# One hybrid-trunk kernel: gate/up groups on pairs of PSUM banks, row scale moved to the end

## The chip, the cores and the metric

The kernel runs on one core of one Trainium2 chip. Its time is the device time of one execution in microseconds; the kernel before took 948.93 us in the median of three runs (948.30 to 949.33). The profile is of one execution of its own. PE is the matrix engine, DVE the vector engine, ACT the scalar engine, POOL the general one; SP only issues DMAs.

## The reference

Two layers over 256 tokens of width 1024, in float32. Each layer has a feed-forward block (FFN), a mixer (attention inside the stream and into 256 memory rows) and a second FFN, with a residual each:

```python
def rmsnorm(x, g):
    y = x * lax.rsqrt(jnp.mean(x * x, axis=-1, keepdims=True) + EPS)
    return y * g

def swiglu(h, w_gate, w_up, w_down):
    return (jax.nn.silu(h @ w_gate) * (h @ w_up)) @ w_down

for i in range(DEPTH):                              # 2 layers
    x = x + 0.5 * swiglu(rmsnorm(x, ffn1_norm[i]), ...)   # 1024 -> 2816 -> 1024
    ...                                             # mixer: in-projection, attention, out-projection
    x = x + 0.5 * swiglu(rmsnorm(x, ffn2_norm[i]), ...)
```

The row factor of the norm, one number r for each token, commutes with the products: silu(r * (xg @ w_gate)) * (r * (xg @ w_up)) is what the FFN needs, and a factor of a row may also be put on after the down product.

## The kernel before

The 256 tokens are two blocks (`tb`) of 128. Every weight is split into a float32r high part and a remainder (L367 on ACT, L385 on DVE), and a product of float32 accuracy is three passes over PE: high x high, high x low, low x high (L542, L545, L548 in `dense`, L565 and L571 in `two_phases`). Normed activations are split likewise. Some products of the FFN are done by a seven-product scheme (`product`, `pair_sums`, `seven`) to save passes.

The order of all work is written out by a small planner, `Flow`: threads are generators that give up control until a planned time or a condition, and instructions are emitted in the order in which the planner runs them. That order is each engine's program order; on the chip an engine runs its queue in that order, and semaphores make an instruction wait for its inputs and for the last readers of what it overwrites. The planner counts resources. A resource is given back, in its count, at the moment the last reader is emitted.

An FFN runs over 11 groups of 256 hidden columns. `plain_chunk` (L845) computes gate and up of a group for both blocks: 512 columns in one PSUM bank per block, 24 passes each. It takes two banks and spawns `evac`. Two neighbouring groups of every FFN go through the seven-product scheme instead and reach `evac` as sums in SBUF; so 4 x 9 = 36 groups are plain and 8 are not. `evac` (L719) does for each block a silu on ACT with scale r (L728), the product with the up half on DVE with scale r (L731) and a 32x32 block transpose on DVE (L739). Then the group goes through DRAM to bring hidden columns onto the partitions (L745, L751) and is split again (L760, L762). The down products sum into four accumulator banks (`Acc`, `down`); `finish` (L688) adds them into x with the factor 0.5 (L694), `seven_sums` (L805) and `end_sums` (L975) add the rest. `prep_rstd` (L674) makes r, ending in a power on POOL (L585).

PSUM has eight banks of 128x512 float32. `banks` is a count of eight, each use is a tile of a pool of eight buffers, and the pool decides which buffer a tile gets. In the mixer many short uses follow one another: scores (`S`), transposed probabilities (`ptp`, in `p_transpose`, L1492), outputs (`AV`), transposed outputs and queries (`otp`, `qmtp`, `qktp`), and between them the projections (`pj`). `p_transpose` emits ACT's copy, gives its bank and returns, and the next head's call takes a bank:

```python
            nc.scalar.copy(out=pt.rearrange("p a b c -> p (a b) c"), in_=tp[:, 0:2 * nb, :])
            t = flow.act(2 * nk)
            banks.give()
```

Of the kernel before, what the change touches and what calls it, by code (L numbers as in the profile page):

```python
# [20 lines left out]
P = 128  # L21
# [144 lines left out]

@with_exitstack
def kernel(
# [34 lines left out]
    def bank(name, shape=(P, 4, P)):  # L203
        return banks.take(list(shape), F32, name)
# [39 lines left out]
    def gain_columns():  # L244
        grow = const.tile([NGC - 16, P], F32, name="grow")
        for src, r0 in ((mix_norm, GC_MIX), (mem_norm, GC_MEM), (ffn2_norm, GC_FFN2)):
            later(grow[r0 - 16:r0, :], src.rearrange("l (k p) -> (l k) p", p=P))
        for src, r0, n in ((mem_q_norm, GC_MQ, 2), (mem_k_norm, GC_MK, 2), (a_q_norm, GC_AQ, 1),
                           (a_k_norm, GC_AK, 1)):
            for j in range(2):  # L250
                later(grow[r0 - 16:r0 - 16 + n, j * HD:(j + 1) * HD], src)
        later(grow[GC_SUB - 16:GC_SUB - 15, :], b_subln)
        yield from loaded()
        yield banks.has()
        tp = bank("gps")
# [3 lines left out]
        banks.give()  # L259
# [329 lines left out]
    class Xt:  # L589
        def __init__(self, keep=False):  # L590
            self.h = [xtp.tile([P, KT, P], F32R, tag=f"xh{tb}", name=f"xh{tb}") for tb in range(2)]
            self.l = [xtp.tile([P, KT, P], F32R, tag=f"xl{tb}", name=f"xl{tb}") for tb in range(2)]
            self.ss = [sm.tile([P, 2], F32, tag="xss", name="xss", bufs=4) for _ in range(2)]
            self.r = [sm.tile([P, 1], F32, tag="xr", name="xr", bufs=4) for _ in range(2)]
            self.t, self.th = ([[None] * KT for _ in range(2)] for _ in range(2))
# [6 lines left out]
    def prep_half(xt, tb, hf, gc, wait=0.0):  # L602
        yield banks.has()
        tp = bank("xtp")
        for k in range(4):
            t = turn(tp[:, k, :], xs[tb][:, hf * 512 + k * P:hf * 512 + (k + 1) * P])
        yield t
        yield lambda: len(first_gain) > 0 and g2.left > 0
        y = g2.take([P, 4, P], F32, "y")
        ks = slice(hf * 4, hf * 4 + 4)  # L610
        g = gcol[:, gc + hf * 4:gc + hf * 4 + 4]
        nc.vector.tensor_tensor(out=y, in0=tp, in1=g.unsqueeze(2).broadcast_to([P, 4, P]), op=ALU.mult)
        banks.give()
        yield flow.dve(512)
        yield from prep_rest(xt, tb, hf, y, wait)
# [72 lines left out]
    def finish(acc, tb, xt, gc, half, by_dram=False):  # L688
        for hf in range(2):
            sl = slice(hf * 512, (hf + 1) * 512)  # L690
            yield lambda: acc.t[tb][hf] is not None
            yield acc.t[tb][hf]
            if half:
# [4 lines left out]
            banks.give()  # L698
# [12 lines left out]

    def ffn(l, nm, xt, gc_next):
# [6 lines left out]
        def evac(g, ps, end, gives=None):  # L719


            hb = None
            for tb in range(2):
                yield lambda: end[tb] is not None and xt.rt[tb] is not None
                yield end[tb]
                yield g2.has(3)
                sil = g2.take([P, 256], F32, "sil")
                nc.scalar.activation(sil, ps[tb][:, 0:256], AF.Silu, scale=xt.r[tb])  # L728
                yield flow.act(256)
                h = g2.take([P, 256], F32, "h")  # L730
                nc.vector.scalar_tensor_tensor(out=h, in0=ps[tb][:, 256:512], scalar=xt.r[tb], in1=sil,  # L731
                                               op0=ALU.mult, op1=ALU.mult)
                t = flow.dve(256, 0.06)
                g2.give()
                (gives or (banks, banks))[tb].give()
                if hb is None:
                    hb = g2.take([P, 4, 2, 2, 32], F32, "hb")
                yield t
                nc.vector.transpose(out=hb[:, :, tb].rearrange("p b f j -> p f b j"),  # L739
                                    in_=h.rearrange("p (f b i) -> p f b i", f=2, b=4))  # L740
                t = flow.dve(256, 0.05)
                g2.give()
# [62 lines left out]
        def seven_sums(ms, t):  # L805

            def into_x(tb, hf, v):
                sl = slice(hf * 512, (hf + 1) * 512)
                nc.vector.scalar_tensor_tensor(out=xs[tb][:, sl], in0=v, scalar=0.5, in1=xs[tb][:, sl],
                                               op0=ALU.mult, op1=ALU.add)  # L810
                flow.dve(512)
# [10 lines left out]
            banks.give()  # L822
# [5 lines left out]
            banks.give()  # L828
# [5 lines left out]
            banks.give()  # L834
# [4 lines left out]
            banks.give()  # L839
# [5 lines left out]
        def plain_chunk(g, c, tbs, ks=range(4)):  # L845
            if g not in open_:
                flow.until(banks.has(2))
                open_[g] = [bank(f"gu{tb}", (P, 512)) for tb in range(2)], [None, None]
                flow.spawn(evac(g, *open_[g]))
            ps, end = open_[g]  # L850
            for tb in tbs:
                if len(tbs) == 1:
                    t = two_phases(ps[tb], xt, tb, plan[l, nm, "gu"][g, c], range(4 * c, 4 * c + 4), c == 0, c == 1)
                    if c == 1:
                        end[tb] = t
                    continue
                for k in ks:
                    kk = 4 * c + k
                    t = dense(ps[tb], xt.h[tb][:, kk, :], xt.l[tb][:, kk, :], lambda: xt.t[tb][kk],
# [32 lines left out]
        def pair_sums():  # L892
# [10 lines left out]
            banks.give()  # L903
# [5 lines left out]
            banks.give()  # L909
            plus(w, u2, pb["m5"])  # L910
            banks.give()
# [3 lines left out]
            banks.give()  # L915
            for m, (g, tb), x in (("m3", (1, 0), w), ("m2", (0, 0), u), ("m4", (0, 1), u2)):
# [3 lines left out]
                banks.give()  # L920
                pps[g][tb], pend[g][tb] = x, t

        def product(m):
# [5 lines left out]
            if m == "m1":  # L929
                flow.spawn(pair_sums())  # L930
                for e in range(2):
                    flow.spawn(evac(pair + e, pps[e], pend[e], (g2, g2)))
# [42 lines left out]
        def end_sums(t):  # L975
# [4 lines left out]
            for q, queue in enumerate((nc.sync, nc.scalar)):  # L980
# [9 lines left out]
                nc.vector.scalar_tensor_tensor(out=xs[1][:, part], in0=ps, scalar=0.5, in1=xs[1][:, part],  # L990
# [29 lines left out]
        for tb in range(2):  # L1020
            flow.spawn(finish(acc, tb, nxt, gc_next, True, (l, nm) == (0, 1)))
# [135 lines left out]
    def memory_kv(l):  # L1157
# [7 lines left out]
        def evac(ps, tb, t):  # L1165
# [4 lines left out]
            banks.give()  # L1170
# [157 lines left out]
    def mixer(l, xt, gc_next):  # L1328
# [40 lines left out]
        def qk_evac(c):  # L1369
            def run(ps, tb, t):  # L1370
# [4 lines left out]
                banks.give()  # L1375
# [30 lines left out]
                if tb == 0:  # L1406
# [10 lines left out]
                    banks.give()  # L1417
# [5 lines left out]
                else:  # L1423
# [3 lines left out]
                    banks.give()  # L1427
# [3 lines left out]
        def v_evac(ps, tb, t):  # L1431
# [4 lines left out]
            banks.give()  # L1436
# [3 lines left out]
        def vq_evac(ps, tb, t):  # L1440
# [8 lines left out]
            banks.give()  # L1449
# [8 lines left out]
            banks.give()  # L1458
            qm[1][tb] = t

        def o_transpose(o, tb, grp, gain):
# [16 lines left out]
            banks.give()  # L1478
# [13 lines left out]
        def p_transpose(src, nk, flipped=False):  # L1492
# [10 lines left out]
            banks.give()  # L1503
# [6 lines left out]
        def attn_soft(passes, done, vsrc, vready, grp, tb, bias_t, nk):  # L1510
# [5 lines left out]
            for e in range(2):  # L1516
# [4 lines left out]
                if bias_t is not None:  # L1521
# [5 lines left out]
                    banks.give()  # L1527
# [6 lines left out]
            for e in range(2):  # L1534
# [6 lines left out]
                if bias_t is None:  # L1541
                    banks.give()
# [23 lines left out]
            av = bank("AV", (P, 4, P))[:, 0:2, :]  # L1566
# [14 lines left out]
            banks.give()  # L1581
            ott[grp][tb] = t

        def attn_diff(passes, done, vsrc, vready, grp, tb, nk):
# [14 lines left out]
            for e in range(2):  # L1599
# [6 lines left out]
                banks.give()  # L1606
# [18 lines left out]
            av = bank("AV", (P, 4, P))[:, 0:2, :]  # L1625
# [21 lines left out]
            banks.give()  # L1647
# [93 lines left out]
        for tb in range(2):  # L1741
            flow.spawn(finish(acc, tb, nxt, gc_next, False))
# [16 lines left out]
    def start_gain():  # L1759
# [5 lines left out]
        banks.give()  # L1765
# [4 lines left out]
        warm(1)  # L1770

# [9 lines left out]
    banks.give()  # L1781
# [68 lines left out]
```

## Time and profile before

| | us |
|---|---|
| median of 3 runs | 948.93 |
| profiled execution, its own time | 948.83 |
| its span, first to last instruction | 947.0 |
| PE busy | 940.3 |
| PE weight loads busy | 773.2 |
| DVE busy | 829.7 |
| ACT busy | 590.8 |
| POOL busy | 108.6 |

The own time of the profiled execution is 1.8 us longer than its span and 0.1 us under the median. A busy share says how much of the span an engine had an instruction in work. A product of PE is pipelined: it shows some 0.39 us, while the next one starts 0.23 us after it. So for PE the spacing of the starts is to be read, not the length. Layer 0's mixer lies at about 220 to 310 us, layer 1's at about 670 to 775 us; the rest is FFN.

### The profile page before, as it was taken

Reading aid. Unit: us, or ns where it says so; the run is one execution under the profiler, and the core shown is the slowest. Engines: PE = TensorE matmul, PEld = TensorE weight load, DVE = VectorE, ACT = ScalarE, POOL = GpSimd, SP = SyncE. Lnnn points to the kernel's source line nnn. Section 1 sums busy time; section 2 is a strip of 40 time slices with the busy share of each in tenths; the row PEclk is TensorE's granted clock in tenths of the full one; section 3 lists DMA queues with packets and bytes.
Section 4 is the critical chain, followed back from the end, with each engine's and each line's share of the span. In section 5 each row is a group of like instructions: output and inputs, shape, how many; then the busy total and the mean of one; then the engine's idle time right before and its main releaser. Section 6 shows DMA issues by size and latency. Waiting matters only on the chain. (4 is left out here: it accounts for less than half of the span.)

```text
span 947.0 us, 13323 instructions
## 1 busy us (share of the span) xinstructions
PE 940.3 (99%) x4456; PEld 773.2 (82%) x4456; DVE 829.7 (88%) x1501; ACT 590.8 (62%) x1126; POOL 108.6 (11%) x160
## 2 busy tenths in 40 slices
PE   9999999999999999999999999999999999999998
PEld 7888888887878888888888888888887788888887
DVE  6989988888777889989889899796999899998995
ACT  6656666677786746647546656563777765655671
POOL 0000038731210000000000000000334100000000
PEclk9999999999999999999999999999999999999999
DMA  9968799688525486896847679775632367589561
GB/s 296 284 212 250 228 325 329 231 268 254 178 90 164 121 258 210 266 291 225 259 143 217 214 233 290 236 252 173 203 130 76 131 219 225 188 260 329 183 217 47
DMA packets 172574, 206.13 MB, mean 218 GB/s; under 512 B 10265, under 2 KB 147290, under 8 KB 172506
## 3 DMA queue, kind: packets, MB, share of 16 engines
q1 hardware_dynamic: 169498, 202.92, 67.0%
q10 hardware_dynamic: 3008, 2.37, 0.8%
q8 instruction: 35, 0.57, 0.2%
q14 instruction: 33, 0.27, 0.1%
HBM read 190.04 MB, written 15.20 MB: 217 GB/s over the span
## 5 line engine op out<-in xcount | busy, mean ns | idle before, releaser
L367 ACT CAST hi<-raw 128x512 fp32r<-128x512 f32 (+1 forms) x466 | 334.8, 770 | 152.4 <-DMA raw<-in_ffn_w_up_dram 45.7
L385 DVE TENSOR_TENSOR lo<-raw,hi 128x512 fp32r<-128x512 f32 (+1 forms) x466 | 392.2, 877 | 23.1 <-ACT hi L367 22.5
L548 PE MATMUL gu<-hi,xl 128*128 128x512 f32 x528 | 206.0, 390 | 0.0
L542 PE MATMUL gu<-hi,xh 128*128 128x512 f32 x528 | 206.0, 390 | 0.0
L545 PE MATMUL gu<-lo,xh 128*128 128x512 f32 x528 | 205.8, 390 | 0.0
L545 PEld LDWEIGHTS gu<-lo,xh 128*128 128x128 f32 x528 | 99.2, 188 | 21.0 <-DVE lo L385 0.4
L548 PEld LDWEIGHTS gu<-hi,xl 128*128 128x128 f32 x528 | 99.3, 188 | 21.0 <-DVE xl L654 0.4
L542 PEld LDWEIGHTS gu<-hi,xh 128*128 128x128 f32 x528 | 99.4, 188 | 20.4
L548 PE MATMUL acc<-hi,ht 128*128 128x512 f32 x270 | 105.6, 391 | 0.0
L542 PE MATMUL acc<-hi,ht 128*128 128x512 f32 x270 | 105.1, 389 | 0.0
L545 PE MATMUL acc<-lo,ht 128*128 128x512 f32 x270 | 105.1, 389 | 0.0
L367 ACT CAST hi<-wsum 128x512 fp32r<-128x512 f32 x83 | 49.0, 620 | 40.0 <-DVE wsum L379 37.0
L548 PE MATMUL pj<-hi,xl 128*128 128x512 f32 x160 | 63.9, 400 | 0.0
L545 PE MATMUL pj<-lo,xh 128*128 128x512 f32 x160 | 63.6, 397 | 0.0
L542 PE MATMUL pj<-hi,xh 128*128 128x512 f32 x160 | 63.5, 397 | 0.0
L545 PEld LDWEIGHTS acc<-lo,ht 128*128 128x128 f32 x270 | 50.7, 188 | 10.6
L542 PEld LDWEIGHTS acc<-hi,ht 128*128 128x128 f32 x270 | 50.7, 188 | 10.4
L548 PEld LDWEIGHTS acc<-hi,ht 128*128 128x128 f32 x270 | 50.7, 188 | 10.4
L585 POOL TENSOR_TENSOR xr<-v,nhalf 128x1 f32<-128x1 f32 x12 | 8.6, 719 | 429.6 <-DVE v L583 429.6
L385 DVE TENSOR_TENSOR lo<-wsum,hi 128x512 fp32r<-128x512 f32 x83 | 53.7, 676 | 0.0
L728 ACT ACTIVATE sil<-gu,xr 128x256 f32<-128x256 f32 x72 | 33.8, 469 | 24.7 <-PE gu L548 23.1
L585 POOL TENSOR_TENSOR hf<-v,nhalf 128x8 f32<-128x8 f32 (+1 forms) x20 | 32.1, 1607 | 83.2 <-DVE v L583 74.1
(244 smaller groups left out, 1531.5 us busy)
## 6 DMA issues: line engine op xcount, KB each, us to landing
raw<-in_ffn_w_down_dram SPq DMA_DIRECT2D x176, 256.0 KB, 4.4
raw<-in_ffn_w_gate_dram SPq DMA_DIRECT2D x82, 512.0 KB, 4.6
raw<-in_ffn_w_up_dram SPq DMA_DIRECT2D x82, 512.0 KB, 5.2
raw<-in_w_in_dram SPq DMA_DIRECT2D x32, 512.0 KB, 5.1
hd<-hb SPq DMA_DIRECT2D x44, 256.0 KB, 4.9
hr<-hd SPq DMA_DIRECT2D x44, 256.0 KB, 5.1
raw<-in_w_out_dram SPq DMA_DIRECT2D x8, 1024.0 KB, 4.9
raw<-in_w_mem_kv_dram SPq DMA_DIRECT2D x4, 1024.0 KB, 9.0
```

The source lines that it names most:

```text
L367: nc.scalar.copy(out=it.part(0, q, w), in_=src())
L385: nc.vector.tensor_sub(it.part(1, q, w), src(), it.part(0, q, w).bitcast(F32))
L542: nc.tensor.matmul(out=ps, lhsT=xh, rhs=wh, start=start, stop=False)
L545: nc.tensor.matmul(out=ps, lhsT=xh, rhs=wl, start=False, stop=False)
L548: nc.tensor.matmul(out=ps, lhsT=xl, rhs=wh, start=False, stop=stop)
L585: nc.gpsimd.tensor_tensor(out=dst, in0=v[:, :n], in1=nhalf[:, :n], op=ALU.pow)
L728: nc.scalar.activation(sil, ps[tb][:, 0:256], AF.Silu, scale=xt.r[tb])
```

## The change

The eight banks become one tile, and a class `Banks` hands them out by number. A single take and a take of two neighbours have a rule each. Each give names its bank.

```diff
+class Banks:
+    def __init__(self, tile):
+        self.tile, self.free, self.held = tile, list(range(8)), {}
...
+    def has_pair(self):
+        return lambda: any(b + 1 in self.free for b in self.free)
...
+    def take(self, shape):
+        beside = lambda b: (b - 1 in self.free) + (b + 1 in self.free)
+        b = min(self.free, key=lambda b: (beside(b), self.free.index(b)))
...
+    def take_pair(self):
+        age = self.free.index
+        b = min((b for b in self.free if b + 1 in self.free), key=lambda b: max(age(b), age(b + 1)))
+        return self._hold(self.tile[:, b:b + 2, :], (b, b + 1))
+
+    def give(self, view):
+        self.free += self.held.pop(id(view))[1]
...
-    pp = ctx.enter_context(tc.tile_pool(name="pp", bufs=8, space=PSUM))
+    pp = ctx.enter_context(tc.tile_pool(name="pp", bufs=1, space=PSUM))
...
-    banks = Slots(flow, pp, "ps", 8)
+    banks = Banks(pp.tile([P, 8, 512], F32, name="banks"))
```

A plain group takes a pair. Both silus write halves of one SBUF tile, then one product and one transpose of 512 elements per partition do both blocks, and the pair is given back. The product has no scale any more. The paired groups, whose inputs are sums in SBUF, keep two products and two transposes, also without the scale.

```diff
-                flow.until(banks.has(2))
-                open_[g] = [bank(f"gu{tb}", (P, 512)) for tb in range(2)], [None, None]
+                flow.until(banks.has_pair())
+                open_[g] = banks.take_pair(), [None, None]
...
+                for tb in range(2):
+                    yield lambda: end[tb] is not None and xt.rt[tb] is not None
+                    yield end[tb]
+                    if tb == 0:
+                        yield g2.has(3)
+                        sil = g2.take([P, 2, 256], F32, "sil")
+                    nc.scalar.activation(sil[:, tb], ps[:, tb, 0:256], AF.Silu, scale=xt.r[tb])
+                    t = flow.act(256)
+                yield t
+                h = g2.take([P, 2, 2, 4, 32], F32, "h")
+                nc.vector.tensor_mul(h.rearrange("p t f b i -> p t (f b i)"), ps[:, :, 256:512], sil)
+                t = flow.dve(512, 0.06)
                 g2.give()
...
+                banks.give(ps)
+                hb = g2.take([P, 4, 2, 2, 32], F32, "hb")
                 yield t
...
+                nc.vector.transpose(out=hb.rearrange("p b t f j -> p (t f) b j"),
+                                    in_=h.rearrange("p t f b i -> p (t f) b i"))
+                t = flow.dve(512, 0.1)
```

The scale that the product no longer has is put on where the down sums are added to x. `prep_rstd` makes half of r on POOL, and `finish`, `seven_sums` and `end_sums` take that column in place of 0.5.

```diff
+        nc.gpsimd.tensor_scalar(out=xt.rh[tb], in0=xt.r[tb], scalar1=0.5, scalar2=None, op0=ALU.mult)
+        flow.pool(0.25)
...
-                nc.vector.scalar_tensor_tensor(out=xs[tb][:, sl], in0=acc.ps[tb][hf], scalar=0.5, in1=xs[tb][:, sl],
+                nc.vector.scalar_tensor_tensor(out=xs[tb][:, sl], in0=acc.ps[tb][hf], scalar=rh[tb], in1=xs[tb][:, sl],
                                                op0=ALU.mult, op1=ALU.add)
```

The bank of the warm-up products at the start is given after the last of them instead of at once. No product of PE and no DMA is added, removed or reshaped.

## Rows read from the trace of the kernel before

**Rows 1.** The page: busy us, share of the span, instructions; granted clock by slices.

```profile
PE 940.3 (99%) x4456; PEld 773.2 (82%) x4456; DVE 829.7 (88%) x1501; ACT 590.8 (62%) x1126; POOL 108.6 (11%) x160
...
PEclk9999999999999999999999999999999999999999
```

**Rows 2.** Stretches: length, busy us of PE, PEld, DVE, ACT, POOL, clock, DMA.

```profile
20.00:220.00 200.00, 200.00 (x884) 165.32 (x883) 177.07 (x310) 129.06 (x234) 59.00 (x109) 1.00 0.84 269
220.00:310.00 90.00, 88.89 (x560) 71.42 (x559) 71.97 (x203) 63.86 (x164) 11.71 (x7) 1.00 0.51 158
...
670.00:775.00 105.00, 104.62 (x587) 83.91 (x586) 96.06 (x203) 74.49 (x196) 31.99 (x28) 1.00 0.48 157
...
943.40:947.00 3.60, 0.00 (x0) 0.00 (x0) 0.42 (x1) 0.00 (x0) 0.00 (x0) 1.00 0.21 73
```

**Rows 3.** Waits of PE: who waited for whom, total us, times, longest.

```profile
PE qktp L578 <- DVE qkn L1049: 1.1, 1, 1.1
PE S L1487 <- ACT PT L1501: 0.2, 1, 0.2
```

**Rows 4.** Timeline, gate/up and mixer: start, length, engine, line, [idle before <- releaser].

```profile
102.54 0.39 PE L542 MATMUL gu<-hi,xh 128*128 128x512 f32 x1
...
107.75 0.39 PE L548 MATMUL gu<-hi,xl 128*128 128x512 f32 x1
...
221.34 0.74 DVE L1049 SCALAR_TENSOR_TENSOR qkn<-pj,xr,hf 128x512 f32<-128x512 f32 x1
...
222.13 0.44 PE L578 MATMUL qktp<-flip,qkn 128*128 128x128 f32 x2 [1.11 <-DVE qkn L1049]
```

**Rows 5.** Groups by line and shape: count, busy us, mean ns, idle before.

```profile
L728 ACT ACTIVATE sil<-gu,xr 128x256 f32<-128x256 f32 x72 | 33.8, 469 | 24.7 <-PE gu L548 23.1
...
L739 DVE STREAM_TRANSPOSE hb<-h 128x256 f32<-128x256 f32 x88 | 38.1, 435 | 0.1
L731 DVE SCALAR_TENSOR_TENSOR h<-gu,xr,sil 128x256 f32<-128x256 f32 x72 | 34.3, 476 | 7.2 <-ACT sil L728 7.2
...
L694 DVE SCALAR_TENSOR_TENSOR x<-acc,x 128x512 f32<-128x512 f32 x16 | 11.0, 688 | 13.4 <-PE acc L548 13.3
...
L1049 DVE SCALAR_TENSOR_TENSOR qkn<-pj,xr,hf 128x512 f32<-128x512 f32 x12 | 8.9, 742 | 1.3 <-POOL hf L585 1.3
...
L697 DVE TENSOR_TENSOR x<-acc,x 128x512 f32<-128x512 f32 x8 | 5.4, 684 | 2.0 <-PE acc L548 2.0
...
L1074 DVE STREAM_TRANSPOSE mb<-mem 128x256 f32<-128x256 f32 x8 | 4.6, 606 | 0.0
L623 DVE STREAM_TRANSPOSE xb<-x 128x512 f32<-128x512 f32 x4 | 4.4, 1094 | 0.0
...
L1579 DVE TENSOR_TENSOR oT<-AV,oT 128x256 fp32r<-128x256 f32 x10 | 4.2, 418 | 2.8 <-ACT oT L1577 2.8
```

**Rows 6.** Timeline at three places: a bank's reader, and products beside it.

```profile
14.12 0.69 DVE L612 TENSOR_TENSOR y<-xtp,gcol 128x512 f32<-128x512 f32 x1
...
14.39 0.60 PE L578 MATMUL xtp<-ident,x 128*128 128x128 f32 x4
...
269.89 0.59 ACT L1501 COPY PT<-ptp 128x512 f32<-128x512 f32 x1
...
270.07 0.60 PE L578 MATMUL ptp<-flip,pe 128*128 128x128 f32 x4
...
734.78 0.42 DVE L1151 TENSOR_TENSOR q<-qktp,q 128x256 fp32r<-128x256 f32 x1
...
735.13 0.38 PE L578 MATMUL ptp<-ident,pe 128*128 128x128 f32 x2
```

**Rows 7.** POOL: one group by line, and the timeline in layer 1's mixer.

```profile
L1236 POOL TENSOR_SCALAR ropew<-invf,pos_f 128x32 f32<-128x32 f32 x2 | 1.5, 766 | 8.6 <-DVE h L731 8.6
...
677.95 1.89 POOL L1386 TENSOR_TENSOR m<-qkn,ropeS 128x256 f32<-128x256 f32 x2 [1.69 <-issue]
```

**Rows 8.** Timeline, the last add of the kernel.

```profile
943.39 0.42 DVE L990 SCALAR_TENSOR_TENSOR x<-end,x 128x256 f32<-128x256 f32 x1 [0.21 <-PE end L986]
```

More of the change, by code (lines that the diff above doesn't have):

```diff
@@ L203, in bank @@
     def bank(name, shape=(P, 4, P)):
-        return banks.take(list(shape), F32, name)
+        return banks.take(shape)
     g1row = const.tile([16, P], F32, name="g1row")
@@ L594, in __init__ @@
             self.r = [sm.tile([P, 1], F32, tag="xr", name="xr", bufs=4) for _ in range(2)]
+            self.rh = [sm.tile([P, 1], F32, tag="xrh", name="xrh", bufs=4) for _ in range(2)]
             self.t, self.th = ([[None] * KT for _ in range(2)] for _ in range(2))
@@ L717, in ffn, with evac @@
         slow[0] = 0.0
[L719 to L733, printed above, removed]
+        def evac(g, ps, end, summed=False):
+            if summed:
+                for tb in range(2):
+                    yield lambda: end[tb] is not None and xt.rt[tb] is not None
+                    yield end[tb]
+                    yield g2.has(3)
+                    sil = g2.take([P, 256], F32, "sil")
+                    nc.scalar.activation(sil, ps[tb][:, 0:256], AF.Silu, scale=xt.r[tb])
+                    yield flow.act(256)
+                    h = g2.take([P, 256], F32, "h")
+                    nc.vector.tensor_mul(h, ps[tb][:, 256:512], sil)
+                    t = flow.dve(256, 0.06)
+                    g2.give(2)
+                    if tb == 0:
+                        hb = g2.take([P, 4, 2, 2, 32], F32, "hb")
+                    yield t
+                    nc.vector.transpose(out=hb[:, :, tb].rearrange("p b f j -> p f b j"),
+                                        in_=h.rearrange("p (f b i) -> p f b i", f=2, b=4))
+                    t = flow.dve(256, 0.05)
+                    g2.give()
+            else:
+                for tb in range(2):
+                    yield lambda: end[tb] is not None and xt.rt[tb] is not None
+                    yield end[tb]
+                    if tb == 0:
+                        yield g2.has(3)
+                        sil = g2.take([P, 2, 256], F32, "sil")
+                    nc.scalar.activation(sil[:, tb], ps[:, tb, 0:256], AF.Silu, scale=xt.r[tb])
+                    t = flow.act(256)
+                yield t
+                h = g2.take([P, 2, 2, 4, 32], F32, "h")
+                nc.vector.tensor_mul(h.rearrange("p t f b i -> p t (f b i)"), ps[:, :, 256:512], sil)
+                t = flow.dve(512, 0.06)
@@ L827, in seven_sums @@
             yield plus(u, u, ms[2])
-            banks.give()
+            banks.give(ms[2])
             yield calm
@@ L833, in seven_sums @@
             yield plus(u, u, ms[3])
-            banks.give()
+            banks.give(ms[3])
             yield calm
@@ L838, in seven_sums @@
             yield plus(u, u, ms[1])
-            banks.give()
+            banks.give(ms[1])
             into_x(1, 1, u)
@@ L902, in pair_sums @@
             yield flow.act(512)
-            banks.give()
+            banks.give(pb["m1"])
             yield lambda: "m6" in mt and "m7" in mt
@@ L1169, in evac @@
             kvt[1][tb] = flow.act(256)
-            banks.give()
+            banks.give(ps)
             if tb == 0:
@@ L1416, in run @@
                         t = flow.act(512)
-                    banks.give()
+                    banks.give(tp)
                     yield t
@@ L1435, in v_evac @@
             Vt[0][tb] = flow.act(512)
-            banks.give()
+            banks.give(ps)
         qm = [None, [None, None]]
@@ L1477, in o_transpose @@
             t = flow.dve(256)
-            banks.give()
+            banks.give(tp)
             ott[grp][tb] = t
@@ L1502, in p_transpose @@
             t = flow.act(2 * nk)
-            banks.give()
+            banks.give(tp)
             g2.give()
@@ L1541, in attn_soft @@
                 if bias_t is None:
-                    banks.give()
+                    banks.give(src)
                 pes[e].append(t)
@@ L1580, in attn_soft @@
             t = flow.dve(256)
-            banks.give()
+            banks.give(av)
             ott[grp][tb] = t
@@ L1605, in attn_diff @@
                     t = flow.act(nk, 0.1)
-                banks.give()
+                banks.give(ss[e][0])
             yield t
@@ L1646, in attn_diff @@
             t = flow.dve(256)
-            banks.give()
+            banks.give(av)
             yield t + 0.3
@@ L1764, in start_gain @@
         nc.vector.tensor_copy(gcol[:, 0:16], tp[:, 0, :16])
-        banks.give()
+        banks.give(tp)
         flow.dve(16)
@@ L1770, in start_gain @@
         warm(1)
+        banks.give(wb)
     def start(tb, hf, t):
```

71 lines of the change are left out of this document (40 added, 31 removed).

## The prediction

> **What bounds the kernel now.** I read the page's engine shares first, then the busy time by stage, then PE's waits, then the product stream itself. The shares [rows 1] give PE 99% and DVE 88% of 947.0 us, with the clock at its upper level, 2.4 GHz, in every slice. By stage [rows 2] PE is busy for all of 20 to 220 us, for 88.89 of 90 us in the mixer of layer 0, for 104.62 of 105 us in the mixer of layer 1, and not at all in the last 3.6 us. So the page's PE idle is 6.7 us: 1.1 and 0.4 in the mixers, 3.6 behind the last product, and the rest, 1.6, at the start. PE waits for a compute engine only in the mixers, 1.3 us in all [rows 3].
>
> Busy time can hide gaps where products overlap, so the starts have to be looked at. From 102.54 to 107.75 us there are 24 products, 23 intervals, one every 0.2265 us, with none longer [rows 4]. In gate/up and down PE streams without a gap. There no saved DVE time can reach the end; only what PE itself must wait for can. The number of products and their shapes are the same after the change, so the floor stays and the question is which waits of PE it adds or takes away.
>
> **Part 1, one product and one transpose for two blocks.** A plain group now has two silus on ACT, two scaled products and two block transposes on DVE. The change keeps the silus. There are 36 plain groups (72 products at L731). Products: 72 x 476 ns = 34.3 us [rows 5]. The new one reads 512 elements from PSUM and 512 from SBUF without a column scalar; the nearest row is L697, a sum of 128x512 with one side in PSUM, 684 ns. 36 x 684 ns = 24.6 us, so 9.7 us less. Transposes: 72 x 435 ns = 31.3 us. No row shows this form at 512. From 256 to 512, L1074 and L623 go from 606 to 1094 ns, a ratio of 1.81, but they read with a stride; 435 x 1.81 = 785 ns. Bounds: a slope as of the sums (684 - 418 = 266 ns for 256 more [rows 5]) gives 701 ns; the whole step of L623 over L1074, 488 ns, gives 923 ns. I take 785: 28.3 us, 3.1 less (6.1 less to 1.9 more). The 16 products of the paired groups lose their scalar: at L731's 476 ns against L1579's 418 ns, a sum of 128x256, 16 x 58 ns = 0.9 us less.
>
> **Part 2, the scale at the end.** The 30 adds into x take a column instead of 0.5. L694 takes 688 ns; L1049, of the same kind with a column, takes 742 ns, but it also reads a broadcast operand, so +54 ns is the upper end and 0 the lower. I take half, 0.8 us. DVE in all: -9.7 - 3.1 - 0.9 + 0.8 = -12.9 us, of 829.7. What of it lies on the path: nothing, since PE's stream covers it [rows 2, 4]; without that cover it would be the 12.9 us. One add lies behind the last product, L990 at 943.39 us [rows 8]; +54 ns at most, +0.05 us.
>
> POOL gets 12 small multiplications for the halved scale. The nearest row is L1236, a multiplication by a column, 766 ns [rows 7]; the bounds are 0, if it ends in POOL's idle time, and 0.8 us each for what is queued behind. Queued behind in layer 1's mixer is L1386, and POOL idles 1.69 us ahead of it [rows 7]. It fits, so 0; without this idle time the rotary product, and the transposes that need it, would be 0.8 us later, once per mixer.
>
> **Part 3, who holds which bank.** This is the part that can reach PE. Before, a count says that some bank is free and the pool chooses which. After, the kernel chooses: a single bank is the free one with the fewest free neighbours, and only among equals the one free for longest; a pair is the adjacent two of which the younger is oldest. "Free" starts when the last reader is *written into its queue*, not when it has run. So a bank with no free neighbour can be taken again at once, however fresh, and PE, which runs in order, then stands until the reader has ended.
>
> To price it I listed the takes and gives of the kernel before in program order (245 takes, with the 36 plain groups' two as one pair), let the two new rules choose, and for each bank so chosen compared the end of its last reader with the start of the first product that would write it, both from the trace. In 10 of 245 the reader ends too late. The example: at 270.07 us PE begins the second head's transposes while ACT copies the first head's bank, 269.89 + 0.59 = 270.48 us [rows 6]. In the kernel before these are two banks. By the new rule the second takes the bank that the first has just given, since it stands alone among the free ones. From reader's end to PE's start there is 0.05 us (L1049: 221.34 + 0.74 = 222.08; PE 222.13 [rows 4]). The wait is 270.48 + 0.05 - 270.07 = 0.46 us. The first of the ten is in the start phase, 14.12 + 0.69 + 0.05 - 14.39 = 0.47 us; the last is 734.78 + 0.42 + 0.05 - 735.13 = 0.12 us [rows 6]. Seven of the ten lie between 228 and 302 us, two in the mixer of layer 1. All ten, worked in this way, come to 3.4 us of reader time and 0.5 us of ten releases: 3.9 us, 0.39 us each. Nothing hides them, since PE has no idle time there to give. Bounds: 0, if the new order of the work puts other products between, and twice that, 7.8, if as many again arise; I take 3.9, the value of the order that the trace shows.
>
> A pair also keeps block 0's bank until block 1 is through, 24 products x 0.2265 = 5.4 us longer [rows 4]. In the replay each of the 36 pairs found neighbours free at once, so 0 here (the price if not is a rival below). The warm-up bank is given later, with no reader on another engine: 0.
>
> **The sum.** In the profiled execution's own time: 948.83 + 3.9 + 0.05 + 0 = 952.8 us. The median of the three runs is 948.93, 0.1 above, which I leave out.
>
> **The rivals.** *No new wait* (the other side): the new order of DVE's and ACT's work moves the mixers' bursts, and the banks that are taken early have rested long enough. For it speaks that PE waits for no reader of a bank now [rows 3], and that which burst falls where hangs on the planner's clock. Against it speaks that a head's second transposes follow the first in the code without a wait between. It decides where fewer than 5 of the ten recur: 5 x 0.39 = 1.9 us, 0.2%. Time: 948.9.
>
> *DVE's relief shows*: a shorter DVE queue frees the waits in the mixers, 1.1 us for the normalised queries and 0.2 us for a copy [rows 3]. Time: 948.8 - 1.3 = 947.5, which is still within 0.2%; more only if PE's busy time in the mixers hides gaps that DVE ends, and at the very most 948.8 - 12.9 = 935.9 if DVE and not PE were the bound. Against it: the stream without gaps [rows 4], and that no merged instruction lies in a mixer. The Trainium skill (Perfetto Trace Analysis, Identifying the Most-Contended Engine) says that matmul busy time is no good measure of TensorE and that weight-load busy time is to be taken; that is 82% here, below DVE's 88%, so by that rule DVE would be the most contended and the 935.9 would be due. By that rule the trace does not agree: the 24 starts at even spacing leave no room.
>
> *No neighbours*: a pair is wanted while the free banks are apart. The place is the start of the three later FFNs, when the mixer or down stage still holds accumulators. PE then stands until an accumulator has been added into x: 0.39 - 0.23 + 0.69 + 0.05 = 0.9 us by rows 4 and 5, three times 2.7 us, in addition to the 3.9: 955.5. Against it is the replay. The Trainium skill (PSUM — Partial Sum Buffer, Summary: rules for kernel authors) says to evacuate promptly because PSUM is tight, and the pair does the opposite; by it the sum would be this 955.5.
>
> *All eight banks count as one tile*: if the framework made PE wait for any reader of the one tile, each of 36 groups would cost at least a silu's length and a product's [rows 5], 36 x (0.47 + 0.68) = 41 us, and 0.05: 990. Against it: each use takes its own slice of one bank or of two, and no other is read or written with it; I give it little.
>
> **How the numbers follow.** Forecast 0.49, own range 950.5 to 955.0; no new wait 0.30; DVE's relief 0.10; no neighbours 0.07; one tile 0.04. A measurement of this kernel can tell 0.2%, 1.9 us, from no change. Slower by more: 0.45 of the forecast's 0.49, and 0.07 and 0.04, makes 0.56. Within: 0.04 + 0.30 and 0.03 of the relief, 0.37. Faster by more: the other 0.07 of the relief. The range goes from 947.3, just below the waits that relief could free, to 956.0, above the missing neighbours; it leaves out the one tile, most of the relief and the upper bound of the re-use.
>
> **What would show it.** In the profile after: PE busy total and product spacing in gate/up unchanged; L731's successors 36 at about 0.68 us, transposes 36 at about 0.79 us, DVE near 817 us. PE's waits should name readers of banks, `ptp` behind ACT's `PT` copy above all, some ten rows of 0.1 to 0.7 us between 228 and 302 us, and PE idle there some 3 us more than 1.1. If PE's waits name nothing new and the time stays, the planner's order has spaced the re-use out and Part 3 is wrong. If `gu` products wait, it is the pairs.

## The result, and the profile after

The changed kernel took 953.71 us (median of 6 runs, 953.33 to 954.14) beside 948.83 us for the kernel before (6 runs, 948.30 to 949.33): 1.0050 times as long, with a 95% interval of 1.0039 to 1.0061. It is slower by 4.9 us. The forecast was 952.8 us, with a range of 947.3 to 956.0. The profiled execution took 953.75 us with a span of 952.0 us, so 5.0 us more span than [rows 1].

The page of the kernel after, engine shares and clock:

```profile
PE 942.2 (99%) x4456; PEld 773.4 (81%) x4456; DVE 821.2 (86%) x1429; ACT 590.6 (62%) x1126; POOL 115.2 (12%) x172
...
PEclk9999999999999999999999999999999999999999
```

DVE has 8.5 us less work than in [rows 1] and 72 instructions fewer, and the span is longer all the same. The clock stayed at 2.4 GHz. The busy time by stage, with columns as in [rows 2]:

```profile
20.00:220.00 200.00, 200.00 (x883) 165.34 (x882) 174.02 (x291) 128.20 (x232) 61.02 (x113) 1.00 0.82 267
220.00:310.00 90.00, 87.71 (x549) 69.77 (x548) 71.86 (x204) 64.59 (x165) 11.87 (x8) 1.00 0.50 161
...
670.00:775.00 105.00, 102.65 (x574) 81.48 (x573) 93.54 (x201) 72.70 (x191) 31.69 (x28) 1.00 0.47 151
```

From 20 to 220 us PE is still busy all the time. PE's idle time in the two mixers went from 1.1 and 0.4 us [rows 2] to 2.3 and 2.35 us. In both it shows as fewer instructions inside the same window, 549 for 560 and 574 for 587, because PE is late. PE runs the same instructions in the same order in both kernels, so the n-th product of one can be set against the n-th of the other. Its delay grows by 0.84 us up to 25 us (0.3 of it ahead of 12 us, where the products still start every 0.42 us up to 10.55 us instead of up to 8.85, though the granted clock reads 1.00 there; where this stretch ends varies from kernel to kernel), by nothing further in the gate/up and down stages of all four FFNs, by 1.72 us in layer 0's mixer and by 2.73 us in layer 1's: 5.29 us at the last product. The waits of PE in the kernel after (columns as in [rows 3]; every bank is now called `banks`, so the line and the releaser have to tell the use):

```profile
PE banks L619 <- ACT pe L1666: 1.7, 2, 1.1
PE banks L619 <- DVE qkn L1112: 1.4, 1, 1.4
PE banks L1842 <- POOL ident masks.py:199: 1.3, 1, 1.3
PE banks L619 <- ACT PT L1564: 0.5, 2, 0.3
PE banks L1634 <- DVE nm L1586: 0.4, 1, 0.4
PE banks L619 <- DVE y L654: 0.3, 1, 0.3
PE banks L583 <- ACT qk L1474: 0.2, 1, 0.2
PE banks L619 <- ACT pe L1601: 0.2, 1, 0.2
```

Two of these are no news: the wait for the queries `qkn` answers to the 1.1 us of [rows 3], and the one for POOL's identity at the start is 1.4 us long in the kernel before too. Each of the others, seen at its place, names an instruction that has just read a bank. L619 is `transpose_into`'s product (L578 before), and what it is made to wait for by ACT's `pe`, the exponentials of the scores, is no input of it. The timeline of the kernel after shows four such places, two gate/up products, and three neighbours on DVE:

```profile
14.40 0.69 DVE L654 TENSOR_TENSOR y<-banks,gcol 128x512 f32<-128x512 f32 x1 [0.31 <-PE banks L619]
14.43 0.39 PE L586 MATMUL banks<-lo,xh 128*128 128x512 f32 x1
...
15.15 0.44 PE L619 MATMUL banks<-ident,x 128*128 128x128 f32 x2 [0.33 <-DVE y L654]
...
102.70 0.39 PE L583 MATMUL banks<-hi,xh 128*128 128x512 f32 x1
...
107.91 0.39 PE L589 MATMUL banks<-hi,xl 128*128 128x512 f32 x1
...
109.47 0.42 DVE L775 TENSOR_TENSOR h<-gu_u,sil 128x256 f32<-128x256 f32 x1
109.80 1.22 DVE L426 TENSOR_TENSOR lo<-raw,hi 128x1024 fp32r<-128x1024 f32 x1
110.94 0.44 DVE L781 STREAM_TRANSPOSE hb<-h 128x256 f32<-128x256 f32 x1
...
289.22 0.59 ACT L1564 COPY PT<-banks 128x512 f32<-128x512 f32 x1 [1.07 <-PE banks L619]
289.26 0.40 PE L586 MATMUL banks<-lo,oT 128*128 128x512 f32 x1
...
289.86 0.33 PE L619 MATMUL banks<-ident,qmn 128*128 128x128 f32 x1 [0.21 <-ACT PT L1564]
...
742.02 0.40 PE L583 MATMUL banks<-hi,oT 128*128 128x512 f32 x1
...
743.29 0.20 ACT L1666 ACTIVATION_READ_ACCUMULATOR pe<-banks,nm 128x1 f32 x1
743.55 0.33 PE L619 MATMUL banks<-ident,o 128*128 128x128 f32 x1 [1.13 <-ACT pe L1666]
...
745.21 0.21 ACT L1666 ACTIVATION_READ_ACCUMULATOR pe<-banks,nm 128x1 f32 x1
...
745.47 0.33 PE L619 MATMUL banks<-ident,qmn 128*128 128x128 f32 x1 [0.55 <-ACT pe L1666]
```

Each wait is the same figure: the reader's end, and 0.05 to 0.06 us behind it the product (289.22 + 0.59 = 289.81, product at 289.86). What it costs PE is read from start to start, against the regular 0.23 us: 15.15 - 14.43 - 0.23 = 0.49 us at the start of the kernel, 0.38 us at 289.86, and 743.55 - 742.02 - 0.23 = 1.30 us at the largest. There are ten such places, at 15, 264, 282, 290, 705, 738, 744, 745, 756 and 758 us, 0.23 to 1.30 us each, 5.2 us in all; with 0.3 us more for `qkn` and the 0.3 at the start that is 5.8, of which small gaps of the kernel before that are gone give back 0.5. The 24 products from 102.70 to 107.91 us still start every 0.2265 us, as in [rows 4].

### The profile page after: what moved, and what is told of

Read it like the earlier page. It is cut to its first block, busy times and chain, and to the rows that moved or that the text cites. A ratio compares the mean times of both kernels' runs of the same rounds, so it can differ in the third digit from the quotient of the medians.

```text
span 952.0 us, 13254 instructions
## 1 busy us (share of the span) xinstructions
PE 942.2 (99%) x4456; PEld 773.4 (81%) x4456; DVE 821.2 (86%) x1429; ACT 590.6 (62%) x1126; POOL 115.2 (12%) x172
## 4 chain that ended last, share of the span: by engine, by line
PE 91%; DVE 5%; ACT 2%; DMA 2%; issue 1%; SPq 0%; ACTq 0%; DVEq 0%
PE banks L589 27%; PE banks L583 27%; PE banks L586 27%; PE banks L619 3%; PE banks L606 2%; DVE lo L426 1%; PE banks L1550 1%; PE banks L612 1%; PE banks L1634 1%; DMA raw<-in_w_in_dram 1%; DMA kr<-kd 1%; ACT hi L408 0%; DVE nm L1659 0%; DMA x<-in_x_dram 0%; DVE m L1452 0%
## 5 line engine op out<-in xcount | busy, mean ns | idle before, releaser
L426 DVE TENSOR_TENSOR lo<-raw,hi 128x512 fp32r<-128x512 f32 (+1 forms) x466 | 391.2, 877 | 37.6 <-ACT hi L408 37.6
L583 PE MATMUL banks<-hi,xh 128*128 128x512 f32 x736 | 288.7, 392 | 0.3 <-ACT qk L1474 0.2
L589 PE MATMUL banks<-hi,xl 128*128 128x512 f32 x736 | 288.7, 392 | 0.0
L586 PE MATMUL banks<-lo,xh 128*128 128x512 f32 x736 | 288.2, 392 | 0.0
L583 PEld LDWEIGHTS banks<-hi,xh 128*128 128x128 f32 x736 | 138.7, 188 | 28.9 <-ACT qk L1474 0.7
L586 PEld LDWEIGHTS banks<-lo,xh 128*128 128x128 f32 x736 | 138.6, 188 | 28.8 <-DVE lo L426 0.4
L589 PEld LDWEIGHTS banks<-hi,xl 128*128 128x128 f32 x736 | 138.5, 188 | 28.5 <-issue 0.2
L589 PE MATMUL banks<-hi,ht 128*128 128x512 f32 x270 | 105.6, 391 | 0.0
L583 PE MATMUL banks<-hi,ht 128*128 128x512 f32 x270 | 105.1, 389 | 0.0
L586 PE MATMUL banks<-lo,ht 128*128 128x512 f32 x270 | 105.1, 389 | 0.0
L586 PEld LDWEIGHTS banks<-lo,ht 128*128 128x128 f32 x270 | 50.7, 188 | 10.7
L589 PEld LDWEIGHTS banks<-hi,ht 128*128 128x128 f32 x270 | 50.7, 188 | 10.4
L583 PEld LDWEIGHTS banks<-hi,ht 128*128 128x128 f32 x270 | 50.7, 188 | 10.2
L426 DVE TENSOR_TENSOR lo<-wsum,hi 128x512 fp32r<-128x512 f32 x83 | 53.3, 682 | 2.8 <-ACT hi L408 2.7
```

The costliest lines, as they stand in the source:

```text
L426: nc.vector.tensor_sub(it.part(1, q, w), src(), it.part(0, q, w).bitcast(F32))
L583: nc.tensor.matmul(out=ps, lhsT=xh, rhs=wh, start=start, stop=False)
L586: nc.tensor.matmul(out=ps, lhsT=xh, rhs=wl, start=False, stop=False)
L589: nc.tensor.matmul(out=ps, lhsT=xl, rhs=wh, start=False, stop=stop)
```

## The experiments

The theory is that of the prediction's Part 3: the whole loss is the choice of banks, since a product that is given a freshly read bank waits for its reader (W in the expectations). Two rivals explain the same 4.9 us without it (O and P there): that the merged instructions move ACT's and DVE's work about, or that the pairs hold banks that others need. In e2, e3 and e5 to e7 every engine has the instructions of the kernel after in the same order, and in e1 those of the kernel before, so that in each only bank numbers differ. The first four runs stand beside 948.72 us for the kernel before (15 runs), the last four beside 948.99 us (27 runs).

### e1: the rule alone, in the kernel before

The kernel before gets the class `Banks` with the new rule for single banks. There are no pairs, no merged instructions and no moved scale: each block of a group takes a single bank.

```diff
-    banks = Slots(flow, pp, "ps", 8)
+    banks = Banks(pp.tile([P, 8, 512], F32, name="banks"))
...
+        beside = lambda b: (b - 1 in self.free) + (b + 1 in self.free)
+        b = min(self.free, key=lambda b: (beside(b), self.free.index(b)))
```

> The kernel before, with the new rule for single banks and nothing else of the change: two products, two transposes, scale at the product, two single banks per group. Each engine has the same instructions in the same order as in the kernel before; only the bank numbers differ. Theory W (PE waits for the last reader of a bank that was taken again too early): 948.8 + 3.9 = 952.7 us, with PE waits at the ten places of the replay (14, 229, 262, 270, 280, 287, 291, 302, 717, 735 us). Rival O (the time comes from the changed order and load of DVE, ACT and POOL): 948.8 us. Rival P (it comes from pairs that keep block 0's bank longer): 948.8 us, since there are no pairs here.

Measured: 961.82 us (961.36 to 962.02), 1.0135 times the kernel before (1.012 to 1.015). The rivals' 948.8 is out. The choice of banks makes the kernel slower with nothing else changed. But the loss is 13.1 us, not 3.9, and PE's waits say where the rest lies:

```profile
PE banks L583 <- DVE h L772: 4.6, 3, 3.3
PE banks L619 <- ACT pe L1647: 1.7, 2, 1.1
```

The expectation took the prediction's replay, in which gate/up uses are pairs and follow the pair rule, "the younger is oldest". Here they are singles, and the rule gives a product the bank of the group before while its scaled product on DVE has yet to run. Replayed afterwards with singles, the takes show 17 early re-uses and 17.8 us, which is nearer but well above the measured loss; no run shows this sum. Set product against product, 8.8 of the 13.1 us fall into the gate/up and down stages, 3.65 into the two mixers, and the rest at the start and the end. Two of the waits in layer 1's mixer are the row for `pe`, which is not the rule's alone, as e2 will show. The largest wait is at 414 us, and something follows it. First the timeline of e1, then its windows (columns as in [rows 2]):

```profile
410.59 0.39 PE L589 MATMUL banks<-hi,xl 128*128 128x512 f32 x1
414.31 0.79 PE L583 MATMUL banks<-hi,xh 128*128 128x512 f32 x1 [3.34 <-DVE h L772]
...
417.04 0.63 PE L583 MATMUL banks<-hi,xh 128*128 128x512 f32 x1
417.46 0.63 PE L586 MATMUL banks<-lo,xh 128*128 128x512 f32 x1
```

```profile
412.00:416.00 4.00, 1.69 (x4) 1.40 (x5) 3.85 (x9) 3.75 (x8) 0.00 (x0) 0.64 1.02 318
416.00:420.00 4.00, 4.00 (x11) 3.05 (x11) 4.00 (x6) 0.00 (x0) 0.00 (x0) 0.51 0.43 145
420.00:424.00 4.00, 4.00 (x19) 3.31 (x18) 0.74 (x2) 1.24 (x3) 0.00 (x0) 1.00 0.87 281
```

After 414.31 - 410.59 - 0.23 = 3.5 us without a product the granted clock is 0.64 and then 0.51, the lower of the two levels, 1.2 GHz, and the products start every 0.42 us instead of every 0.23 until 419.6 us. Compared with the kernel before, PE loses 6.27 us at this place: the 3.5 us of the wait and 2.75 us at the lower clock.

### e2 and e3: the kernel after with the oldest, and with the youngest free bank

```diff
     def take(self, shape):
-        beside = lambda b: (b - 1 in self.free) + (b + 1 in self.free)
-        b = min(self.free, key=lambda b: (beside(b), self.free.index(b)))
+        b = self.free[0]
```

e3 has `self.free[-1]` in its place. The pairs, the merged instructions and the moved scale stay.

> The kernel after, with one line changed: a single take gets the bank that is free for longest, whatever its neighbours. Pairs, merged product and transpose, and the scale stay; each engine's instructions and their order are those of the kernel after. Theory W: nearly all of the 4.9 us come back; the same replay with this rule leaves two early re-uses, 0.6 us, so 949.4 us (948.5 to 950.0). Rivals O and P: 953.7 us, since order, load and pairs are unchanged.

> The kernel after, with a single take getting the bank given back last: the suspected cost made larger. Theory W: the replay with this rule finds some 40 early re-uses, 22 us if each counts in full, less where one wait gives the next reader time; 948.8 + 22 = 971 us at most, 960 to 971 us. Rivals O and P: 953.7 us.

Measured: e2 951.32 us (950.27 to 952.73), 1.0027 times the kernel before (1.0015 to 1.0040); e3 962.19 us (960.62 to 963.10), 1.0138 times (1.0123 to 1.0153). Both move the time by the choice of a single bank alone, which supports W; e3 is inside the range expected. But e2 gives back only half, and that is a miss: 949.4 was due by W. PE's waits in e2:

```profile
PE banks L618 <- DVE qkn L1111: 1.8, 1, 1.8
PE banks L618 <- ACT pe L1665: 1.7, 2, 1.1
```

The waits for `PT` are gone, as they should be, and the wait for the exponentials `pe` is still there at its full 1.7 us. The oldest bank should be the best rested one. Here there was no better one on the list, so the question is when a bank enters it.

The kernel before shows the answer. This is its timeline at the same transposes:

```profile
739.29 0.47 DVE L1049 SCALAR_TENSOR_TENSOR qmn<-pj,xr,hf 128x256 f32<-128x256 f32 x1
...
739.82 0.44 PE L578 MATMUL otp<-ident,o 128*128 128x128 f32 x2
```

There `otp` follows the last reader of the projection's bank `pj` by 0.06 us (739.29 + 0.47 = 739.76). In the kernel after that bank is not on the list yet. `head_norm` emits its last reader, gives up control, and only when it is resumed does its caller call `banks.give`. So the list gets the bank one step of the planner late; in the step between, the count is right that one bank is free, but it is the bank of a score product whose exponential is still in ACT's queue. This is a second theory (W2): the rule and the late entry both cost.

### e4: the moved scale alone, in the kernel before

```diff
+        nc.gpsimd.tensor_scalar(out=xt.rh[tb], in0=xt.r[tb], scalar1=0.5, scalar2=None, op0=ALU.mult)
...
-                nc.vector.scalar_tensor_tensor(out=h, in0=ps[tb][:, 256:512], scalar=xt.r[tb], in1=sil,
-                                               op0=ALU.mult, op1=ALU.mult)
+                nc.vector.tensor_mul(h, ps[tb][:, 256:512], sil)
```

and the column `rh` in place of 0.5 in the three adds.

> The kernel before, with the scale moved alone: the product without a scale, half of r made on POOL, the column at the adds into x; banks from the pool as before, two products and two transposes. Theory W: 948.8 us plus 0.05 for the last add, so 948.9 us (948.3 to 949.5). Rival O: some of the 4.9 us, up to 953.7, if POOL's 12 small operations or the slower adds hold something up.

Measured: 948.32 us (948.04 to 948.84), 0.9996 times the kernel before (0.9987 to 1.0005). Part 2, with its 12 POOL operations, costs nothing that can be measured.

### e5 and e6: projection banks enter the list when their last reader is emitted

Both put the two projection banks on the list in `head_norm`, right behind its last instruction; the planner's count of free banks stays as it is, so the order of the work does not change. e5 takes the oldest bank, e6 keeps the rule of the kernel after.

```diff
+    def read(self, view):
+        view, bs = self.held[id(view)]
+        self.free += bs
...
-        yield flow.dve(nh * HD, 0.06)
+        t = flow.dve(nh * HD, 0.06)
+        if whole is not None:
+            banks.read(whole)
+        yield t
```

> As e2 (oldest free bank first), and the banks of the projections are entered as free when their last reader is emitted, in head_norm, instead of a planner step later; the planner's count is as before, so each engine has the instructions and order of the kernel after. Theory W2 (beside the rule for singles, a projection bank that is given late leaves only the bank of a score product whose exp is still running, and the transposes at 742 us wait 1.5 us for it): 951.3 - 1.9 = 949.4 us (948.7 to 950.0), with no wait of PE for an exp at 742 us. Rival (what is left of e2 over the kernel before is the changed load of DVE, ACT and POOL): 951.3 us.

> The kernel after with its own rule for single banks, and the projections' banks free when their last reader is emitted, as in e5; the fourth corner beside the kernel after, e2 and e5. Theory W2: the wait at 742 us goes, some re-uses stay: 953.7 - 1.9 = 951.8 us (951 to 953). Rival: 953.7 us.

Measured: e5 948.87 us (948.28 to 949.30, 11 runs), 0.9998 times the kernel before (0.9989 to 1.0007). e6 953.11 us (952.56 to 953.76), 1.0042 times (1.0028 to 1.0055). PE's waits in e5, and its timeline at the transposes `otp`:

```profile
PE banks L1854 <- POOL ident masks.py:199: 1.3, 1, 1.3
PE banks L628 <- DVE qkn L1121: 1.2, 1, 1.2
PE banks L595 <- DVE lo L435: 0.5, 1, 0.5
PE banks L1646 <- DVE nm L1598: 0.4, 1, 0.4
```

```profile
739.42 0.47 DVE L1121 SCALAR_TENSOR_TENSOR qmn<-banks,xr,hf 128x256 f32<-128x256 f32 x1
...
739.95 0.44 PE L628 MATMUL banks<-ident,o 128*128 128x128 f32 x2
```

The wait for `pe` is gone, the transposes follow the projection's reader as they did before, and the time is that of the kernel before. So the merged product, the merged transpose, the pairs and the moved scale together neither cost nor give anything that can be measured, and W2 holds. One early re-use that costs time is left, the last row: 0.5 us at 280 us, where even the oldest bank had just been read, against 0.4 us that this kernel's start happens to be shorter (the row for `lo` lies in the start, at 8.8 us). Another, at 735 us, costs 0.2 us and is given back a few products later.

The bank numbers in the two programs show why the bank at 280 us was fresh. `Acc` takes four accumulators at once, and the new class names their banks at the take. Two of the four write their first product only at 281.36 and 282.06 us, and one of these holds a bank that was last read at 276.57 us, while the output `AV`, due at 280.21 us, gets a score bank that is read until 280.14 us. The pool of the kernel before settles a bank only when its use is first written, and there `AV` got a bank last read at 276.88 us. No run isolates this third difference.

e6 missed its expectation on size: the 1.7 us wait is gone there too, but the time is hardly below that of the kernel after and 4.2 us above e5 (953.11 - 948.87), because other early re-uses came:

```profile
PE banks L629 <- ACT PT L1577: 0.9, 4, 0.3
PE banks L629 <- DVE y L664: 0.9, 1, 0.9
```

```profile
271.71 0.59 ACT L1577 COPY PT<-banks 128x512 f32<-128x512 f32 x1
...
272.35 0.33 PE L629 MATMUL banks<-flip,pe 128*128 128x128 f32 x1 [0.30 <-ACT PT L1577]
```

This is the prediction's own example of [rows 6], the second head's transposes behind the first head's copy. e6 holds early re-uses at 15, 230, 264, 272, 283, 291, 294, 306, 721 and 739 us, which are the replay's ten places, moved by the delay that has built up. Its 4.2 us are the replay's 3.9. The replay had put banks on the list at their last reader, as e6 does and the kernel after does not.

The four kernels that differ in these two points alone, in us:

| | late entry | early entry |
|---|---|---|
| rule of the kernel after | 953.71 | 953.11 |
| oldest free bank | 951.32 | 948.87 |

The two costs do not add up. The rule costs 2.4 us with late entry and 4.2 with early; the late entry costs 2.45 us with the oldest bank and 0.6 under the rule. The 0.6 is hardly clear of the noise: as ratios to the kernel before, 1.0050 and 1.0042 have overlapping intervals. Of the 2.45, the two waits for `pe` make 1.8 (1.08 and 0.71 us, product against product), and some 0.6 stand at the wait for `qkn`, which is not shown to come from the entry.

### e7: rested banks first, then the rule

Early entry as in e6, with a time for each bank from the planner's clock. A bank whose reader has ended at least 0.5 us ago comes first, and only among those are the neighbours counted. The age of a pair goes by these times too.

```diff
+        wait = lambda b: max(0.0, self.ready[b] + REST - self.flow.now)
-        b = min(self.free, key=lambda b: (beside(b), self.free.index(b)))
+        b = min(self.free, key=lambda b: (wait(b), beside(b), self.ready[b]))
```

> As e5, but a single take gets a bank whose last reader has ended by the planner's clock 0.5 us ago, if there is one, and among those the one with the fewest free neighbours; else the one whose reader ends first. Theory W2: neighbours may be looked at, if only among rested banks: 949.4 us, up to 950.5 where the planner's clock is wrong by more than 0.5 us. If looking at neighbours is bad in itself: as e6, 951.8 us.

Measured: 949.97 us (949.10 to 951.55), 1.0010 times (1.0001 to 1.0019), inside what was expected. The rule does little harm where it chooses among rested banks; it gains nothing over the oldest bank either.

### e8: e5 with the merged product issued twice

```diff
                 nc.vector.tensor_mul(h.rearrange("p t f b i -> p t (f b i)"), ps[:, :, 256:512], sil)
+                nc.vector.tensor_mul(h.rearrange("p t f b i -> p t (f b i)"), ps[:, :, 256:512], sil)
```

> As e5, with the merged product of each of the 36 groups issued twice, the second time over the same result: 36 x 0.684 = 24.6 us more for DVE and nothing else. Theory that PE's stream is the bound: the time of e5 within 1 us, 949.4 us, since DVE has 12% idle time. Rival that DVE is the most contended engine: up to 24.6 us more, 974 us.

Measured: 951.53 us (949.99 to 954.32, 10 runs), 1.0026 times (1.0017 to 1.0035), 2.7 us above e5. DVE is busy for 844.5 us, 23.3 more than in e5. A kernel bound by DVE would have lost all of the 23.3 us; it lost a ninth, so DVE does not bound the whole. But 2.7 us is more than the 1 us expected of a kernel bound by PE. Set product against product, the profiled execution loses 2.67 us between 195 and 209 us, 0.5 at the start and 0.2 elsewhere, and PE's waits name the remainders of weights:

```profile
PE banks L595 <- DVE lo L435: 2.0, 2, 1.3
```

The two waits are at 203 and 205 us. In e5 PE has no wait in this stretch (its 0.5 us for `lo` lie at 8.8 us), so with the smaller load the splits of weights keep up with PE there. In that one stretch added DVE work reaches the end; the DVE work that the change saves gives nothing, as e5 shows.

No version was found that is measurably faster than the kernel before: e4 and e5 lie within 0.1% of it, with intervals that contain 1.

## Why the prediction held, and where it did not

**The bound** held. PE's spacing in gate/up is unchanged, and 8.5 us less DVE work was worth nothing (e5, 0.9998). The rival that counted on DVE's relief is out, and with it the 935.9 us by the rule of the Trainium skill (Perfetto Trace Analysis, Identifying the Most-Contended Engine; of the two measures that it names for TensorE, MFU and weight-load busy time, the prediction took the second). Weight loads stay below DVE in e5, 82% to 87%, much as in [rows 1], so by that rule DVE would still be the bound. The runs do not agree: 23.3 us more DVE work cost 2.7 us. One row of the kernel before was left out of the first step, which had PE wait for a compute engine only in the mixers. It is as long in the kernel after, to 0.1 us:

```profile
PE warm L1778 <- POOL ident masks.py:199: 1.4, 1, 1.4
```

**Part 1** held on the path, with one term mis-sized and one error of counting. The groups of the kernel after, by line and shape (columns as in [rows 5]):

```profile
L802 DVE STREAM_TRANSPOSE hb<-h 128x512 f32<-128x512 f32 x36 | 25.4, 705 | 0.2
L796 DVE TENSOR_TENSOR h<-banks,sil 128x512 f32<-128x512 f32 x36 | 24.6, 684 | 1.0 <-ACT sil L792 1.0
L738 DVE SCALAR_TENSOR_TENSOR x<-banks,xrh,x 128x512 f32<-128x512 f32 x16 | 12.0, 748 | 12.5 <-PE banks L589 12.4
```

The product took the 684 ns that the sum with one side in PSUM takes. The transpose took 705 ns, not 785: the lower bound, the slope of the sums, was right, and the strided rows were the wrong neighbours. The durations of all DVE instructions, count times mean over all groups, fell by 13.7 us, from 928.1 to 914.4, near the 12.9 forecast. But the busy time fell by 8.5 us only, to 821.2 and not 817. The forecast subtracted durations from a busy time, and DVE's instructions overlap: in the timeline above L775 lasts 0.42 us and the next one starts 0.33 us after it, and L426 lasts 1.22 us and is followed after 1.14. In the kernel before the durations add up to 928.1 us in 829.7 us of busy time, 0.066 us of overlap for each of 1501 instructions. 72 instructions fewer take 72 x 0.066 = 4.7 us of overlap with them; 13.7 - 4.7 = 9.0 us, close to the 8.5. The Trainium skill (Perfetto Trace Analysis, Optimizing Scalar/DVE Operations) says as much: the latency in a profile is about twice the busy overhead, some 60 ns on SBUF, because the acknowledgement of the write overlaps with the next instruction. The trace agrees, with its 66 ns.

**Part 2** held: nothing on the path (e4). The adds with a column took 748 ns against 688 [rows 5], 60 ns more, a little over the upper end of 54. POOL's halving took less than its bound of 766 ns, in the groups of the kernel after:

```profile
L722 POOL TENSOR_SCALAR xrh<-xr 128x1 f32<-128x1 f32 x12 | 6.1, 511 | 1.0
```

**Part 3** named the right mechanism, the right sign and nearly the right sum: 3.9 us forecast, 4.9 measured. e1 and e2 show that the choice of single banks costs by itself, and e6 against e5 that the rule costs 4.2 us where the list is as the replay had it. The composition was wrong. Of the ten places foreseen five recur in the kernel after: the start, three of the seven in layer 0's mixer, and one of the two in layer 1's. Five others came, all in layer 1's mixer, the two largest of them (1.30 and 0.71 us) behind score banks that the replay never chose. The failed step is "*Free* starts when the last reader is written into its queue". That is so for most banks, and it was so in the pool of the kernel before, where by the bank numbers in its program 275 of 281 uses got the bank whose last reader had been written longest ago. It is not so for the projections' banks, whose `give` stands behind a `yield` of `head_norm`. With five recurring the count stood just at the point from which the rival without a new wait would have decided. That the sum came out nevertheless is partly luck: five missing places, some 1.9 us at 0.39 each, met five unforeseen ones, 0.32 + 1.30 + 0.71 + 0.34 + 0.47 = 3.1 us. PE's idle time in layer 0's mixer grew by 1.2 us instead of the 3 foreseen, and in layer 1's by 2.0 us, where two places, at the mean of 0.39 us, were foreseen. Two of the five that recur, at 282 and 738 us, are not the rule's: they stand in e2 and e5 as well.

**No neighbours and one tile** did not occur. No `gu` product waits in the kernel after, and the timeline of gate/up has no gap. The rule of the Trainium skill to evacuate promptly because PSUM is tight (PSUM — Partial Sum Buffer, Summary: rules for kernel authors) would have made the longer-held pair cost; here it cost nothing, since e5 holds the same pairs and takes 948.87 us.

What stays open: what it would cost or save to name the accumulators' banks only at their first product, as the pool does (e5, 280 us), and why the wait for `qkn` at the start of layer 0's mixer is 0.3 us longer in the kernel after and 0.7 us longer in e2, while in e5 it is 1.2. It lies between 1.0 and 1.8 us in all ten profiles, 1.3 in e4, where the pool chooses the banks. No run isolated either.

## What to carry to other kernels

When a kernel names its own buffers, the order in which free ones are handed out is part of the schedule: on an engine that has no slack, take the longest-free one first and put a buffer on the list at the very moment when its last reader is emitted, ahead of any point at which control is given up. A buffer that is named long before its first use takes a rested one away from a use that is due at once. To price a new rule, replay it over the old trace with exactly the places where the new code gives, not with those where the old one did. And before shortening an engine's work, double it: if the time moves little, the saving is worth nothing, and the place where it does move shows where that engine is just in time.

## What the runs showed of the hardware

- One wait of PE of 3.5 us, behind a stream without gaps, was followed by a granted clock of 0.64 and 0.51 and products every 0.42 us, until 419.6 us; it cost 2.75 us beside the wait itself (e1). Waits of 0.2 to 1.4 us in the kernel after and of 1.8 us in e2 left the granted clock at 1.00 in the windows around them.
- DVE's instructions overlap by some 0.066 us each, so a merged pair saves less busy time than the difference of the durations.
- A block transpose of 128x512, in the form that this kernel has, took 705 ns against 435 ns for 128x256 [rows 5]: merging two saves 165 ns, where the rows with a stride gave 85.
- 60 ns is what a column in place of a constant added to an add of 128x512, 748 against 688 ns.
